# Nearest 2x upsampling on one core: two loads and eight of nine stores move from the SyncE and ScalarE queues to GpSimd, as single packets

## The chip, the cores and the metric

The kernel runs on one core of a Trainium2 chip. The metric is the device time of one execution in microseconds (us), as the median of several runs. A core has compute engines, each with its own instruction queue: TensorE (PE), VectorE (DVE), ScalarE (ACT), GpSimd (POOL) and SyncE (SP). Here only DVE computes. Data move between the off-chip memory (HBM) and the on-chip memory (SBUF, 128 partitions) by 16 DMA engines, which all queues share: an instruction on SP, ACT or POOL only issues a transfer, and a semaphore tells when it has landed.

## The reference

```python
def setup_inputs():
    batch, channels, h, w = (16, 64, 64, 64)
    return {'x': np.random.randn(batch, channels, h, w).astype(np.float32), 'scale_factor': 2}

def reference(x, scale_factor):
    ...
    for i in range(new_h):
        for j in range(new_w):
            src_i = i // scale_factor
            src_j = j // scale_factor
            result[:, :, i, j] = x[:, :, src_i, src_j].copy()
```

Every input value is written four times, twice along the width and twice along the height. 16.78 MB are read and 67.11 MB are written; nothing is calculated.

## The kernel before, in words

The input is seen as 65,536 image rows of 64 floats (256 bytes). Each of the 128 partitions holds 512 consecutive rows, so a partition's share of any run of rows is one contiguous piece of HBM. The output has the same split: one input row becomes two output rows of 128 floats, 1,024 contiguous bytes.

All of the input lies in SBUF at once, in `xt`. It comes in three loads, called A, B and C here: rows 0 to 31, 32 to 287 and 288 to 511 of each partition (`cuts`, lines 195 to 197). All three are issued by SP. The helper `begin_before_barrier` takes the first `EARLY` = 3 transfers of SP out of the body of the program and puts them ahead of SP's part in the barrier at the program's start, so that they are issued at once.

Then come nine groups of rows (`rows`, line 181: 54, 38, 54, 60, 54, 62, 64, 62 and 64). For each, DVE copies the rows into an expanded tile `u`, reading each value twice along the width and each row twice (`expanded`, lines 199 to 202), and one transfer stores `u` to HBM. Copies and stores are numbered 0 to 8 here. Copy 0 is cut in two: its first row alone (line 216), then the other 53 rows (line 217).

There is no separate memory for all the tiles. `u` lies by turns at the start of one large buffer `mem` and just below the unread part of the input (`at`, line 208). So copy n+2 writes where the tile of store n lay, and must wait until store n has landed. Copy 0 waits for load A (its first row) and B; copies 5 and later read rows of load C.

The issuing queue is SP for loads A, B, C and stores 0, 1 and 8, and ACT for stores 2 to 7 (line 218). The transfers of one queue are taken up in their order. Each queue's instruction waits until DVE has finished the tile that it stores.

A transfer over 128 partitions is spread over 16 DMA engines, eight partitions to each. A partition's piece is one packet here: the page counts 1,728 packets for 12 transfers, which is 128 of data and 16 small ones for the semaphore to each.

The helper `close_early` rearranges the end of the program: all engines meet in the closing barrier once their instructions are issued; GpSimd waits for all transfers but the last and clears the semaphores; SP waits only for the last store and resets its semaphore.

Of the kernel before, what the change touches and what calls it, by code (L numbers as in the profile page):

```python
# [6 lines left out]

EARLY = 3  # L10


def begin_before_barrier(nc):
# [5 lines left out]
    sp = mybir.EngineType.SP  # L19
    loads = [i for i in body.instructions if i.engine == sp][:EARLY]  # L20
    for load in loads:
# [132 lines left out]
@with_exitstack  # L154
def kernel(
    ctx: ExitStack,
    tc: tile.TileContext,
    x: bass.AP,
    scale_factor: int,
    out: bass.AP,  # L160
):
    nc = tc.nc
    nc.at_finalize(begin_before_barrier)
    nc.at_finalize(close_early)
    P = nc.NUM_PARTITIONS
    s = int(scale_factor)
    B, C, H, W = x.shape
    R = B * C * H // P
    fdt = x.dtype

    xp = x.rearrange("b c h w -> (b c h) w").rearrange("(p r) w -> p r w", p=P)
    op = out.rearrange("b c (h hd) w -> (b c h) (hd w)", hd=s).rearrange(
        "(p r) w -> p r w", p=P
    )

    rows = [54, 38, 54, 60, 54, 62, 64, 62, 64]
    GROW = s * s
    FREE = 79
    WF = FREE * GROW * W
    assert sum(rows) == R
    mem_pool = ctx.enter_context(tc.tile_pool(name="mem", bufs=1))
    LEAD = 32
    whole = mem_pool.tile([P, LEAD + WF + R * W], fdt, name="mem")
    mem = whole[:, LEAD:]
    xt = mem[:, WF:].rearrange("p (r w) -> p r w", r=R)  # L190

    HEAD = 32
    cuts = [0, HEAD, R // 2 + HEAD, R]
    for lo, hi in zip(cuts, cuts[1:]):
        nc.sync.dma_start(out=xt[:, lo:hi], in_=xp[:, lo:hi])  # L197

    def expanded(r0, r1):
        return (  # L200
            xt[:, r0:r1].unsqueeze(2).unsqueeze(4).to_broadcast([P, r1 - r0, s, W, s])
        )

    r0 = 0
    before = (0, 0)
    for n, k in enumerate(rows):
        size = k * GROW * W
        at = 0 if n % 2 == 0 else WF + r0 * W - size
        assert at >= before[1] or at + size <= before[0]
        before = (at, at + size)  # L210
        u = mem[:, at : at + size].rearrange(
            "p (k a w b) -> p k a w b", k=k, a=s, w=W
        )
        k0 = 1 if n == 0 else 0
        if k0:
            nc.vector.tensor_copy(out=u[:, :k0], in_=expanded(r0, r0 + k0))  # L216
        nc.vector.tensor_copy(out=u[:, k0:], in_=expanded(r0 + k0, r0 + k))  # L217
        issuer = nc.sync if n in (0, 1, len(rows) - 1) else nc.scalar
        issuer.dma_start(out=op[:, r0 : r0 + k, :], in_=u)
        r0 += k  # L220


# [33 lines left out]
```

## Time and profile before

| | us |
|---|---|
| median of 3 runs (196.98 to 197.09) | 197.05 |
| the profiled execution's own time | 197.08 |
| span in the profile | 195.8 |
| DVE busy | 76.9 |
| POOL busy | 0.2 |
| DMA queues' packets (share of 16 engines' span) | 55.0% + 44.2% |
| bytes moved | 83.89 MB, 429 GB/s over the span |

The time is the span and about 1.3 us around it. The span begins with the first instruction, which is the issue of load A. Times of single events below count from there. In the chain of work that ended last, each row gives its start, its length and what it was; a row "DMA" is the time from the issue of a transfer to its landing, as far as an instruction waited for it. In the timeline, each row gives start, length, engine, line, operation and, in brackets, how long the engine had been idle and what ended that. The view by windows gives, for a stretch, the busy time of each engine, the clock of TensorE, the share of the 16 DMA engines' time and the rate; there a packet counts whole at the moment at which it starts, so a stretch in which several packets start has a share above 1.

### The profile page before, as it was taken

The numbers are of one execution on the slowest core, as the hardware profiler recorded it, in microseconds if no ns is written. First come the engines' busy times: TensorE is split into PE (matmuls) and PEld (weight loads), VectorE is DVE, ScalarE is ACT, GpSimd is POOL, SyncE is SP. The second block draws the span as 40 slices with busy tenths as digits, with TensorE's granted clock in tenths as the row PEclk, the third lists the DMA queues.
The fourth block names the chain that finished last, engine by engine and source line by source line (L and its number), as shares of the span: only waits on it lengthen the run. The fifth ranks groups of instructions, "written<-read, shape, count | busy, mean of one in ns | idle before, by whom it ended". The sixth has DMA issues, their size and how long they took to land.

```text
span 195.8 us, 76 instructions
## 1 busy us (share of the span) xinstructions
DVE 76.9 (39%) x10; POOL 0.2 (0%) x4
## 2 busy tenths in 40 slices
DVE  0000099990029287059008805920790079000000
POOL 0000000000000000000000000000000000000000
DMA  9999989989898988999999899999999999999994
GB/s 429 429 429 429 402 375 539 398 362 542 362 435 382 551 373 362 542 402 402 402 537 407 362 542 415 415 415 415 429 429 429 429 415 558 473 435 422 429 429 214
DMA packets 1728, 83.89 MB, mean 429 GB/s; under 512 B 192, under 2 KB 192, under 8 KB 192
## 3 DMA queue, kind: packets, MB, share of 16 engines
q10 hardware_dynamic: 864, 46.66, 55.0%
q1 hardware_dynamic: 864, 37.22, 44.2%
HBM read 16.78 MB, written 67.11 MB: 429 GB/s over the span
## 4 chain that ended last, share of the span: by engine, by line
DMA 61%; DVE 24%; SPq 0%; issue 0%
DMA out_dram<-mem 49%; DVE mem L217 24%; DMA mem<-in_x_dram 12%; SPq L197 0%
## 5 line engine op out<-in xcount | busy, mean ns | idle before, releaser
L217 DVE COPY mem<-mem 128x13824 f32<-128x13824 f32 (+5 forms) x9 | 76.6, 8515 | 84.6 <-DMA out_dram<-mem 65.6
L216 DVE COPY mem<-mem 128x256 f32<-128x256 f32 x1 | 0.3, 293 | 4.8 <-DMA mem<-in_x_dram 4.8
L237 POOL MEMSET const-bfloat16-1.0<- 128x1 bf16 x1 | 0.1, 102 | 0.0
L237 POOL MEMSET const-uint8-127<- 128x1 uint8 x1 | 0.1, 101 | 0.0
L237 POOL MEMSET const-float32-0.0<- 128x1 f32 x1 | 0.1, 98 | 0.2 <-issue 0.2
L237 POOL MEMSET const-float32-1.0<- 128x1 f32 x1 | 0.1, 98 | 0.0
## 6 DMA issues: line engine op xcount, KB each, us to landing
out_dram<-mem ACTq DMA_DIRECT2D x2, 7936.0 KB, 31.6
out_dram<-mem ACTq DMA_DIRECT2D x2, 6912.0 KB, 23.7
out_dram<-mem ACTq DMA_DIRECT2D x1, 7680.0 KB, 26.1
mem<-in_x_dram SPq DMA_DIRECT2D x1, 7168.0 KB, 40.2
out_dram<-mem SPq DMA_DIRECT2D x1, 6912.0 KB, 19.0
out_dram<-mem SPq DMA_DIRECT2D x1, 4864.0 KB, 25.2
mem<-in_x_dram SPq DMA_DIRECT2D x1, 1024.0 KB, 4.8
mem<-in_x_dram SPq DMA_DIRECT2D x1, 23.7
```

What stands on the lines that cost most here:

```text
L216: nc.vector.tensor_copy(out=u[:, :k0], in_=expanded(r0, r0 + k0))
L217: nc.vector.tensor_copy(out=u[:, k0:], in_=expanded(r0 + k0, r0 + k))
L237: nc = _bacc.Bacc("TRN2", target_bir_lowering=False, num_devices=1)
```

## The change

Load A becomes 64 rows and stays on SP. Loads B and C become 224 rows each (64 to 287 and 288 to 511) and are issued by GpSimd, with `single_packet=True`: the eight pieces of each DMA engine form one packet. Stores 0 to 7 are issued by GpSimd too, in the same way. Store 8 stays on SP as it was. ACT issues nothing. `EARLY` becomes 1, since only load A is left ahead of the barrier; GpSimd's loads come after it. The copies on DVE are the same ten instructions. The larger load A now holds all the 54 rows of copy 0, so copy 0 waits for load A alone, and copy 1 is the first to wait for load B.

```diff
-EARLY = 3
+EARLY = 1
...
-    HEAD = 32
-    cuts = [0, HEAD, R // 2 + HEAD, R]
-    for lo, hi in zip(cuts, cuts[1:]):
-        nc.sync.dma_start(out=xt[:, lo:hi], in_=xp[:, lo:hi])
+    HEAD = 64
+    cuts = [0, HEAD, R // 2 + HEAD // 2, R]
+    nc.sync.dma_start(out=xt[:, :HEAD], in_=xp[:, :HEAD])
+    for lo, hi in zip(cuts[1:], cuts[2:]):
+        nc.gpsimd.dma_start(out=xt[:, lo:hi], in_=xp[:, lo:hi], single_packet=True)
...
-        issuer = nc.sync if n in (0, 1, len(rows) - 1) else nc.scalar
-        issuer.dma_start(out=op[:, r0 : r0 + k, :], in_=u)
+        dst = op[:, r0 : r0 + k, :]
+        if n == len(rows) - 1:
+            nc.sync.dma_start(out=dst, in_=u)
+        else:
+            nc.gpsimd.dma_start(out=dst, in_=u, single_packet=True)
```

## The prediction

> **What bounds the kernel now.** I read the page's DMA parts first, then the chain of work that ended last, then the timeline around each store.
>
> ```profile
> q10 hardware_dynamic: 864, 46.66, 55.0%
> q1 hardware_dynamic: 864, 37.22, 44.2%
> HBM read 16.78 MB, written 67.11 MB: 429 GB/s over the span
> DMA 61%; DVE 24%; SPq 0%; issue 0%
> ```
>
> The packets of the two queues fill 55.0% + 44.2% = 99.2% of what 16 DMA engines have in the span. The chain gives DVE 24%, but that is only the way by which the waits lead back; the DMA engines work on underneath. The timeline shows it:
>
> ```profile
> 24.11 19.55 DVE L217 COPY mem<-mem 128x13568 f32<-128x13568 f32 x2 [18.99 <-DMA mem<-in_x_dram]
> 57.46 7.36 DVE L217 COPY mem<-mem 128x13824 f32<-128x13824 f32 x1 [13.80 <-DMA out_dram<-mem]
> 64.85 82.42 ACTq L219 DMA_DIRECT2D out_dram<-mem  x6
> 69.03 8.16 DVE L217 COPY mem<-mem 128x15360 f32<-128x15360 f32 x1 [4.21 <-DMA out_dram<-mem]
> 85.25 7.36 DVE L217 COPY mem<-mem 128x13824 f32<-128x13824 f32 x1 [8.07 <-DMA out_dram<-mem]
> 103.47 8.43 DVE L217 COPY mem<-mem 128x15872 f32<-128x15872 f32 x1 [10.85 <-DMA out_dram<-mem]
> 119.68 8.70 DVE L217 COPY mem<-mem 128x16384 f32<-128x16384 f32 x1 [7.78 <-DMA out_dram<-mem]
> 138.47 8.43 DVE L217 COPY mem<-mem 128x15872 f32<-128x15872 f32 x1 [10.10 <-DMA out_dram<-mem]
> 157.71 8.69 DVE L217 COPY mem<-mem 128x16384 f32<-128x16384 f32 x1 [10.81 <-DMA out_dram<-mem]
> ```
>
> Each copy from 57.46 on starts when an older store lands, so the starts are landings: stores 0 to 6 at 57.46, 69.03, 85.25, 103.47, 119.68, 138.47 and 157.71. Between the first and the last, stores 1 to 6 (332 rows, 43.52 MB) land in 100.25 us: 434 GB/s. The idle time in the brackets is DVE's slack: when copy n is done, store n goes into the queue and the store ahead of it still runs for that long. The smallest such cover is 4.21 us (store 2, issued at 64.85, taken up when store 1 ends near 69). Nothing that DVE does sets the end: the DMA engines do, from the first byte to the last.
>
> So only three things can change the time: what a byte costs inside the engines, what they lose at the start, and a gap if a transfer is not there in time. At the start, and packet by packet:
>
> ```profile
> 0.50:1.00 0.50, 0.00 (x0) 0.00 (x0) 1.00 0.00 0
> 1.00:1.50 0.50, 0.00 (x0) 0.00 (x0) 1.00 1.41 229
> 1.50:2.00 0.50, 0.00 (x0) 0.00 (x0) 1.00 0.49 131
> 2.00:4.00 2.00, 0.00 (x0) 0.00 (x0) 1.00 0.98 414
> 62.48:62.49 0.01, 0.01 (x1) 0.00 (x0) 1.00 26.98 11674
> 192.61:192.62 0.01, 0.00 (x0) 0.00 (x0) 1.00 45.34 19661
> ```
>
> A packet counts whole where it starts, so the last two rows weigh packets. At 62.48, 11674 GB/s x 0.01 us = 116.7 KB are three pieces of store 1 (38 KB); 26.98 x 16 x 0.01 us / 3 = 1.439 us each. At 192.61, 196.6 KB are three pieces of store 8 (64 KB) with 45.34 x 16 x 0.01 / 3 = 2.418 us each. The 26,624 bytes between them take 0.979 us, 36.77 ns per KB of 1,000 bytes; 38,912 bytes at that pace are 1.431 us. Some 8 ns of each packet (within 1 ns, by the last digit) are not bytes.
>
> **The change, part by part.**
>
> *Packets.* Ten transfers (B, C, stores 0 to 7) put eight pieces on each engine. As one packet they would pay the 8 ns once and not eight times: 10 x 7 x 8.1 ns = 0.57 us on every engine, all of it on the path, since the engines never rest. Load A and store 8 keep their eight packets. Bounds: nothing if the 8 ns belong to the piece, and 0.57 us if to the packet. I take the upper end: the two rows show a cost at each boundary, and the change takes the boundary away.
>
> By the Trainium skill's page "DMA: Bandwidth & Descriptors", section "Why small descriptors are slow (HBM only)", a packet costs about three cycles, and packetization saves that but not what belongs to a descriptor. At the 850 MHz that the same page gives in "Where 436 GB/s comes from", three cycles would be 3.5 ns, an estimate of 0.25 us for 70 boundaries, and the sum would be 196.8; the rows show 8 ns, and which part of it is the packet's no row here tells.
>
> *Load A from 32 to 64 rows.* It is first as before. The first 1.05 MB land at 4.83 and A and B together (9.44 MB) at 24.11:
>
> ```profile
> 4.83 0.29 DVE L216 COPY mem<-mem 128x256 f32<-128x256 f32 x1 [4.83 <-DMA mem<-in_x_dram]
> 0.00 0.38 SPq L197
> ```
>
> That is 8.39 MB in 19.28 us, 435 GB/s, so a load A of 2.10 MB lands at 4.83 + 2.41 = 7.2 if nothing gets between. It is the same bytes in the same order and costs nothing.
>
> *Loads B and C on GpSimd, after the barrier.* SP needs 0.38 us for one issue, then the barrier; I put GpSimd's issue at about 0.7. A transfer issued by SP moves its first bytes 1.0 us after its issue (nothing before 1.00 in the windows above). What a GpSimd issue needs no row shows. Its lower bound is SP's 1.0; as its upper bound I take the 2.4 us that load A needs beyond its bytes (4.83 - 2.41). So B's first bytes come between 1.7 and 3.1, while load A keeps the engines busy to about 6.7. The cover is 3.6 us beyond the upper bound; behind it each us costs a us.
>
> *Copy 0* waits for A alone and runs from about 7.5.
>
> ```profile
> L217 DVE COPY mem<-mem 128x13568 f32<-128x13568 f32 x1 | 14.3, 14286 | 19.0 <-DMA mem<-in_x_dram 19.0
> L217 DVE COPY mem<-mem 128x9728 f32<-128x9728 f32 x1 | 5.2, 5226 | 0.0
> ```
>
> Its 53 rows take 14.29 us and the 38 of copy 1 5.23, by the groups by form, so it ends near 22, not at 38.4. Store 0 then lies in the queue behind load C, which ends at 41 as before. This gains nothing, as the engines are full until 41 anyway; what it buys is cover for a slower issue. Copy 1 waits for B (24.1) as DVE's next work, and ends at 29.4.
>
> *Stores 0 to 7 on GpSimd.* Same order, one queue, no store behind a later one's wait: each waits only for its copy, and the one reused load semaphore that store 3 and store 7 also wait for is set long before. An issue slower than ACT's is hidden as long as it takes less than the 4.21 us of store 2's cover less about 1 us of landing; the other stores have 7.8 us or more. Over the upper bound of 2.4 us this holds, so I cost it at nothing. The tiny packet that raises the semaphore is there as before.
>
> *The end.* Store 8 stays on SP, is issued near 166 while store 7 runs, and the engines work both off in either order. GpSimd's clearing is done while store 8 still runs. Nothing.
>
> Sum against the profiled execution (197.08, span 195.8): 197.08 - 0.57 = 196.5. It stands 0.03 above the median of 197.05, so the forecast is **196.5 us**, 0.28% faster. A gain can be larger: between 1.00 and 2.00 the engines move 180 KB where at 414 GB/s it would be 414, a loss of 0.56 us, and a second queue that fills in there could give it back: 196.0.
>
> **The rivals.**
>
> *Load A stuck behind the large packets (slower).* A transfer on a second queue does not wait for the first queue's end. Store 7 went out on ACT, store 8 on SP:
>
> ```profile
> 128.40 18.87 ACTq L219 DMA_DIRECT2D out_dram<-mem  x2
> 166.43 0.33 SPq L219 DMA_DIRECT2D out_dram<-mem  x1
> out_dram<-mem ACTq DMA_DIRECT2D x1, 7936.0 KB, 36.7
> ```
>
> Store 7, issued at 146.9, alone would land 18.7 us (8.13 MB at 434 GB/s) after store 6, at 176.4. It landed at 146.9 + 36.7 = 183.6, so 7.2 us of store 8, three of its 2.42 us packets, went in between: the engines take queues by turns, packet by packet. In the new kernel B's packet on each engine is 57,344 x 8 bytes, 16.9 us at 434 GB/s, and C's the same. If B comes up while packets of A are left, A waits 16.9 us; with two left, it waits for C too, since each turn gives A one packet. Then A lands at 41, copy 0 ends at 55.6, and store 0's bytes come 1.0 to 2.4 us later, with the engines empty from 41: 15.6 us or more. If copy 1 right behind it (5.2 us) also holds GpSimd's issue back, 20.8. Time: 196.5 + 15.6 = 212, up to 218.
>
> For it: A's packets (16 KB, 0.61 us each) run until 6.7, and B comes at 1.7 to 3.1. Against it: the engines choose well ahead. Store 2 was issued at 64.85 into 4.2 us of store 1 and did not delay it at all (69.03 - 57.46 = 11.57 us for 4.98 MB, its own time at 434 GB/s being 11.5); store 8's first packet came only after store 7's sixth, some 4 us after its issue. Counted from 0.7 that gives 4.7, with three packets of A still to be chosen by then if GpSimd's queue is as fast as ACT's, and none if it needs 2 us more. It decides at that point. By my bounds GpSimd's issue takes up to 1.4 us more than SP's, which leaves at most a packet or two to chance; since nothing in the trace decides between these ends, I give the clean start the greater part, but not by much.
>
> The page named above says in "Queues, rings and completion order" that an engine goes round its queues and drains a whole packet before it switches; the trace agrees, by store 7's 36.7 us.
>
> *Store 0's issue waits for DVE.* Only if load A is late, but not behind C: copy 0 would then run from 24.1 to 38.4 as before, copy 1 at once to 43.65, and if GpSimd cannot issue while DVE copies, store 0's bytes start at 44.7 and the engines stand still for 3.6 us: 200.1. It needs A to land after 9.8 (24.1 - 14.3); from about 20 on it costs time. No row here shows a GpSimd issue beside a copy.
>
> It is the rule of the Trainium skill's page "SBUF — State Buffer", section "SBUF: two separate sides", box "The 'DVE blocks DMA' trap (SWDGE)": DVE's fp32 copies lock GpSimd out while it writes descriptors. For stores 1 to 7 the rule would cost nothing here, since DVE's idle times of 4.2 to 13.8 us behind each copy leave room.
>
> *GpSimd's path is slower by itself.* Issue beyond the covers of 3.6 us (load B) or 3.2 us (store 2), or each of its transfers leaving a tenth of a us between itself and the next (ten of them, 1.0 us, which has no cover): 197.5 to 199.
>
> *The 8 ns stay, or the queue eats them.* Then the time is that of before, 197.05.
>
> **How the numbers follow.** This kernel's runs differ by 0.1 us, so 0.2% (0.39 us) is about what can be told from no change. Chances: the clean saving 0.46 (196.0 to 196.65); no net change 0.12; a moderate loss, by the slower path or store 0's wait, 0.23 (197.45 to 201.5); load A behind both packets 0.19 (210 to 218). So faster 0.46, same 0.12, slower 0.42. The likeliest one's own range is 196.0 to 196.7; the range that leaves out the last case and little else is 196.0 to 201.5.
>
> **What would show it.** Right: the first copy of line 218 near 7.5 us and the next near 24; no idle DMA slice; the pieces of stores 0 to 7 at 434 GB/s plus 8 ns per piece less; a span near 195.2. Wrong: the first copy near 24 or 41, and a hole in the DMA row behind 41 us; B's first bytes after 6.7; or the packets' shares adding to what they were, with the span at 195.8. What would make the forecast wrong most surely is load A's place in the turns.

## The result: slower by 0.6%, lost between load C and store 0

The changed kernel takes 198.32 us (198.27 to 198.39), the kernel before 197.07 in the same runs: a ratio of 1.0062, 95% interval 1.005 to 1.0074. The forecast was 196.5 us; its range ran on to 201.5. The span of the profile grew from 195.8 to 197.0 us. First the page of the changed kernel (its DMA packets and queues), then rows of its timeline:

```profile
DMA packets 1728, 83.89 MB, mean 426 GB/s; under 512 B 192, under 2 KB 192, under 8 KB 192
q0 software_dynamic: 1440, 73.40, 86.6%
q1 hardware_dynamic: 288, 10.49, 12.6%
```

```profile
1.31 1.20 POOL L198 DMA_DIRECT2D mem<-in_x_dram  x2 [0.87 <-PEq L255]
13.38 0.29 DVE L217 COPY mem<-mem 128x256 f32<-128x256 f32 x1 [13.38 <-DMA mem<-in_x_dram]
13.59 19.54 DVE L218 COPY mem<-mem 128x13568 f32<-128x13568 f32 x2
28.17 5.08 POOL L223 DMA_DIRECT2D out_dram<-mem  x1 [25.66 <-DVE mem L218]
33.43 0.54 POOL L223 DMA_DIRECT2D out_dram<-mem  x1 [0.18 <-issue]
58.68 7.36 DVE L218 COPY mem<-mem 128x13824 f32<-128x13824 f32 x1 [25.54 <-DMA out_dram<-mem]
66.33 0.53 POOL L223 DMA_DIRECT2D out_dram<-mem  x1 [32.36 <-DVE mem L218]
70.22 8.16 DVE L218 COPY mem<-mem 128x15360 f32<-128x15360 f32 x1 [4.19 <-DMA out_dram<-mem]
158.92 8.69 DVE L218 COPY mem<-mem 128x16384 f32<-128x16384 f32 x1 [10.81 <-DMA out_dram<-mem]
```

Store 0 landed at 58.68 (before: 57.46, 1.22 later), store 1 at 70.22 (1.19 later), store 6 at 158.92 (1.21 later). So nothing is lost after store 0, and the queues' packets still add to 99.2% (86.6% + 12.6%). Windows around the change from loads to stores, called the seam below, show where it went. Each row counts a packet at its start; the first fence is the kernel before, the second the changed one.

```profile
0.00:38.00 38.00, 14.19 (x2) 0.20 (x4) 1.00 0.98 417
38.00:38.90 0.90, 0.86 (x2) 0.00 (x0) 1.00 2.36 1019
40.20:43.00 2.80, 2.80 (x1) 0.00 (x0) 1.00 1.46 632
```

```profile
0.00:38.00 38.00, 19.71 (x3) 7.02 (x8) 1.00 0.98 417
38.00:38.90 0.90, 0.00 (x0) 0.00 (x0) 1.00 3.60 1019
40.20:43.00 2.80, 0.00 (x0) 0.00 (x0) 1.00 0.73 316
```

Up to 38.0 both kernels moved the same: 417 GB/s. In the next 0.9 us the last pieces of load C start in both, one on each of the 16 engines (1019 GB/s x 0.9 us = 16 x 57,344 bytes). Their mean length is the share times the stretch: 2.36 x 0.9 = 2.12 us before, 3.60 x 0.9 = 3.24 after. This stretch on all engines at once is 1.1 of the 1.2 us. Behind it only 16 pieces of store 0 start before 43 (316 GB/s) where 32 did (632).

### The profile page after: what moved, and what is told of

Read it like the earlier page. It is cut to its first block, busy times and chain, and to the rows that moved or that the text cites. A ratio compares the mean times of both kernels' runs of the same rounds, so it can differ in the third digit from the quotient of the medians.

```text
span 197.0 us, 76 instructions
## 1 busy us (share of the span) xinstructions
DVE 76.8 (39%) x10; POOL 10.2 (5%) x14
## 2 busy tenths in 40 slices
DMA packets 1728, 83.89 MB, mean 426 GB/s; under 512 B 192, under 2 KB 192, under 8 KB 192
## 3 DMA queue, kind: packets, MB, share of 16 engines
q0 software_dynamic: 1440, 73.40, 86.6%
q1 hardware_dynamic: 288, 10.49, 12.6%
## 4 chain that ended last, share of the span: by engine, by line
DMA 47%; issue 22%; DVE 13%; POOL 3%; DVEq 0%; POOLq 0%; PEldq 0%
DMA out_dram<-mem 47%; DVE mem L218 13%; POOL out_dram L223 3%; POOL mem L198 1%; DVEq L218 0%; POOLq L223 0%; PEldq L255 0%
## 5 line engine op out<-in xcount | busy, mean ns | idle before, releaser
L223 POOL DMA_DIRECT2D out_dram<-mem x8 | 8.8, 1102 | 137.6 <-DVE mem L218 137.4
L198 POOL DMA_DIRECT2D mem<-in_x_dram x2 | 1.2, 602 | 0.9 <-PEq L255 0.9
```

Of the source, the lines that this page charges most:

```text
L198: nc.gpsimd.dma_start(out=xt[:, lo:hi], in_=xp[:, lo:hi], single_packet=True)
L223: nc.gpsimd.dma_start(out=dst, in_=u, single_packet=True)
```

## The experiments

Three theories at first. P: the packet setting stretches the pieces. G: a load and a store behind each other in GpSimd's queue do it. R: GpSimd has nothing to do with it; the larger load A lets copy 0 end early, store 0 then lies ready while load C is still being read, and that costs 1.2 us.

| kernel | store 0 issued, us | queues of C, store 0 | store 0 landed, us | time, us | ratio to before, 95% |
|---|---|---|---|---|---|
| before | 38.42 | SP, SP | 57.46 | 197.07 | |
| after | 28.17 (to 33.25) | POOL, POOL | 58.68 | 198.32 | 1.005 to 1.0074 |
| multi | 28.27 (to 33.36) | POOL, POOL | 58.66 | 198.22 | 1.0033 to 1.0063 |
| head64_hw | 21.69 | SP, SP | 58.78 | 198.35 | 1.0036 to 1.007 |
| hw_36 | 36.51 | SP, SP | 58.98 | 198.37 | 1.0037 to 1.0067 |
| hw_37 | 37.57 | SP, SP | 58.25 | 197.85 | 1.0027 to 1.0052 |
| hw_38 | 38.83 | SP, SP | 57.63 | 196.99 | 0.9978 to 0.9997 |
| gps_37 | 38.30 | POOL, POOL | 57.41 | 197.01 | 0.9983 to 1.0002 |
| gps_38 | 39.10 | POOL, POOL | 57.60 | 197.48 | 1.0002 to 1.0021 |
| gps_52 | 38.59 | POOL, SP | 58.26 | 197.88 | 1.002 to 1.0045 |
| act01 | 38.33 | SP, ACT | 58.44 | 197.96 | 1.0021 to 1.0045 |
| hw_52 | 38.60 | SP, SP | 57.56 | 197.15 | 0.9987 to 1.0007 |
| early_row | 21.69 | SP, SP | 58.91 | 198.47 | 1.005 to 1.008 |
| loads_sp | 21.89 | SP, POOL | 63.62 | 202.97 | 1.0274 to 1.0305 |
| stores_hw | 28.21 | POOL, SP | 58.46 | 199.45 | 1.0056 to 1.0165 |
| gps_head32 | 40.09 (to 45.18) | POOL, POOL | 62.70 | 202.26 | 1.0211 to 1.0261 |

Each ratio is against runs of the kernel before on the same chip, whose medians lay between 197.07 and 197.36 (single runs between 196.96 and 197.62). The issue and the landing are those of the profiled execution. Where a second time stands, GpSimd's issue took until then.

### The packet setting: multi

```diff
-        nc.gpsimd.dma_start(out=xt[:, lo:hi], in_=xp[:, lo:hi], single_packet=True)
+        nc.gpsimd.dma_start(out=xt[:, lo:hi], in_=xp[:, lo:hi])
...
-            nc.gpsimd.dma_start(out=dst, in_=u, single_packet=True)
+            nc.gpsimd.dma_start(out=dst, in_=u)
```

> The changed kernel without single_packet, all else the same. Theory P (the packet setting causes the stretch of load C's last pieces, 3.3 us where they took 2.1): the hole behind 38.5 us goes, store 0 lands near 57.4, time near 197.1. Theory R (store 0 lies ready in the queue before load C ends, and the change from loads to stores then costs about 1.2 us): nothing changes, 198.3, pieces of the same length as before, load A again at about 13 us. Theory G (a load and a store behind each other in GpSimd's queue cost it): 198.3.

198.22 us, store 0 landed at 58.66, load A at 13.48: the same as with the setting. P falls, and the setting has no effect that these runs show.

### The cuts alone, with no transfer on GpSimd: head64_hw

```diff
-    HEAD = 32
-    cuts = [0, HEAD, R // 2 + HEAD, R]
+    HEAD = 64
+    cuts = [0, HEAD, R // 2 + HEAD // 2, R]
```

> The kernel before with only the cuts changed: load A 64 rows, B and C 224 each, all on SP; no GpSimd transfer. Store 0 is issued near 22 us on SP instead of 38.4. Theory R: the same stretch appears at the end of load C without any GpSimd transfer, time 198.2 to 198.3. Theories P and G: no stretch, 197.0 to 197.1.

The kernel before with nothing but the new cuts takes 198.35 us, ratio 1.0053. Its timeline and windows:

```profile
7.38 14.28 DVE L217 COPY mem<-mem 128x13568 f32<-128x13568 f32 x1
21.69 8.05 SPq L219 DMA_DIRECT2D out_dram<-mem  x2
```

```profile
38.00:38.90 0.90, 0.00 (x0) 0.00 (x0) 1.00 3.78 1019
40.20:43.00 2.80, 0.00 (x0) 0.00 (x0) 1.00 0.73 316
```

Copy 0 ends at 21.7, store 0 is issued 17 us earlier than before, and the last pieces of load C take 3.78 x 0.9 = 3.40 us. The new cuts, set by one number of the change, make the whole loss without GpSimd. P and G fall.

### Loads or stores alone on GpSimd: loads_sp and stores_hw

```diff
 loads_sp (against the changed kernel)
-EARLY = 1
+EARLY = 3
...
-        nc.gpsimd.dma_start(out=xt[:, lo:hi], in_=xp[:, lo:hi], single_packet=True)
+        nc.sync.dma_start(out=xt[:, lo:hi], in_=xp[:, lo:hi])

 stores_hw (against the changed kernel)
-        dst = op[:, r0 : r0 + k, :]
-        if n == len(rows) - 1:
-            nc.sync.dma_start(out=dst, in_=u)
-        else:
-            nc.gpsimd.dma_start(out=dst, in_=u, single_packet=True)
+        issuer = nc.sync if n in (0, 1, len(rows) - 1) else nc.scalar
+        issuer.dma_start(out=op[:, r0 : r0 + k, :], in_=u)
```

> The changed kernel with loads B and C back on SP ahead of the barrier; stores 0 to 7 stay on GpSimd as single packets. Load A should land at 7.2, copy 0 end at 22 and store 0 be issued near 22 without DVE in its way. The engines take queues by turns, so stores 0 may mix with load C. Theory R: a loss of about 1.2 us where C gives way to store 0, or a different one if they mix, 198 or so. Theory G: no load and store share GpSimd's queue, 197.0 to 197.1. Theory P: the stores are still single packets, but load C is not, 197.1.

> The changed kernel with the stores back where they were (0, 1, 8 on SP, 2 to 7 on ACT); loads B and C stay on GpSimd. Load A lands at about 13 again, copy 0 ends at 28, store 0 is issued there on SP while load C is in GpSimd's queue. Theory R: a loss at the change from loads to stores, 198 or so. Theory G: C and store 0 are in different queues, no stretch, 197.1. Theory P: load C is still one packet, 198.3.

Both were meant to separate load C and store 0 into two queues, and both show a second thing with it: the engines then take the two by turns. loads_sp takes 202.97 us (ratio 1.0274 to 1.0305), far from every expectation. Its timeline:

```profile
21.89 0.67 POOL L223 DMA_DIRECT2D out_dram<-mem  x1 [21.45 <-DVE mem L218]
63.62 7.36 DVE L218 COPY mem<-mem 128x13824 f32<-128x13824 f32 x1 [34.36 <-DMA out_dram<-mem]
71.28 0.53 POOL L223 DMA_DIRECT2D out_dram<-mem  x1 [41.17 <-DVE mem L218]
```

Store 0, issued at 21.89, shares the engines with load C and lands at 63.62 where it did at 57.46. Copy 2 waits for it, so store 2 goes out at 71.28 instead of 64.85, when little of store 1 is left:

```profile
25.50:25.80 0.30, 0.30 (x1) 0.00 (x0) 1.00 9.47 2867
70.30:72.30 2.00, 0.68 (x1) 0.53 (x1) 1.00 0.05 19
```

In the 2 us from 70.3 a single piece starts (19 GB/s x 2 us = 38 KB): store 1 is all but over and store 2 not yet there. A transfer that others wait for was slowed by giving its neighbour a turn. The first row is the seam in this run: 15 pieces of load C, just ahead of store 0's first pieces, take 9.47 x 0.3 x 16 / 15 = 3.03 us instead of 2.12. The rest of the 5.6 us (202.97 against 197.36 for the kernel before in the same runs) was not followed up.

stores_hw took 199.45 us in the median, from 198.05 (its profiled execution) to 200.89; that spread is not explained. In the profiled execution store 0 was issued at 28.21 and landed at 58.46, a loss of 1.0 although load C was in another queue. So the loss does not need one queue, which G requires. Its windows show the loss away from the end of load C:

```profile
29.70:30.30 0.60, 0.60 (x1) 0.00 (x0) 1.00 4.70 1529
31.90:32.80 0.90, 0.90 (x1) 0.00 (x0) 1.00 1.82 573
32.80:33.40 0.60, 0.60 (x1) 0.00 (x0) 1.00 1.49 645
```

16 pieces of load C take 4.70 x 0.6 = 2.82 us and the next nine 1.82 x 0.9 x 16 / 9 = 2.91, together 1.1 us more per engine than at 2.12. Then store 0's first pieces come in the third row (seven, of the usual 2.04 us). So in these two runs, as in the changed kernel, the load pieces that are stretched are the one or two just ahead of a large store's first piece on each engine, at the end of load C or in its middle.

### When store 0 is issued: hw_36, hw_37 and hw_38

The kernel before with the cuts of head64_hw; store 0 is held back by copying the first rows of its tile again behind copy 1 (52 rows in hw_36, 52 and 6 in hw_37, 52 and 14 in hw_38). The second copy reads rows that copy 1 has overwritten, so store 0's values are not the reference's in these three and in gps_37 and gps_38; its bytes and their times are those of the same transfer.

```diff
+        if n == 0:
+            held = u
+            r0 += k
+            continue
+        if n == 1:
+            for again in [52]:
+                nc.vector.tensor_copy(out=held[:, :again], in_=expanded(0, again))
+            nc.sync.dma_start(out=op[:, :r0, :], in_=held)
```

> The kernel before with the cuts at 64 and 288 and no GpSimd transfer, but store 0 held back: DVE copies the first 52 rows of its tile a second time behind copy 1, so that store 0 is issued near 36.4 instead of 21.7 us, 1.8 us ahead of the start of load C's last pieces (38.2). Theory R as it stands now (the loss comes when the engines choose store 0's reads while loads are still being read): they choose some 3 to 4 us ahead of the bytes, so the stretch should be whole or nearly: 198.0 to 198.3. Rival R2 (the loss needs a store that lies ready many us ahead): no stretch, 197.1.

> Between hw_36 and hw_38: store 0 is issued near 37.5 us. Its first rows are copied again from memory that copy 1 has overwritten, as in hw_36, hw_38 and gps_38, so the output of store 0 is not the reference's. If the engines choose store 0 as soon as they have asked for the last bytes of load C, and that happens before 38, the stretch is there in whole or on some engines, 197.4 to 198.3; if its descriptors come too late for that, none, 197.0.

> As hw_36, with 14 rows more copied again, so that store 0 is issued near 38.4 us, as in the kernel before. Theories R and R2: the stretch is gone and the time is that of before, 197.0 to 197.4. Rival C (the cuts themselves, 64/224/224 rows, cost the 1.2 us): 198.3 as in head64_hw.

One row of windows each, in the order hw_36, hw_37, hw_38:

```profile
38.00:38.90 0.90, 0.00 (x0) 0.00 (x0) 1.00 3.70 1019
```

```profile
38.00:38.90 0.90, 0.00 (x0) 0.00 (x0) 1.00 3.07 1019
```

```profile
38.00:38.90 0.90, 0.80 (x1) 0.00 (x0) 1.00 2.36 1019
```

The last pieces of load C take 3.33 us when store 0 is issued at 36.51, 2.76 at 37.57 and 2.12 at 38.83. The loss follows the moment of the issue (whole, half and none) within 2.3 us; being ready for many us (R2) is not needed. With the cuts of the slow kernel hw_38 is as fast as the kernel before, so the cuts themselves (rival C) cost nothing.

### The changed kernel with store 0 held back: gps_38 and gps_37

The same insertion in the changed kernel, with `nc.gpsimd.dma_start(..., single_packet=True)`, and 40 rows (gps_38) or 34 rows (gps_37) copied again.

> The changed kernel, with store 0 held back by a second copy of 40 of its rows behind copy 1, so that GpSimd issues it near 38.6 us with DVE idle. Theory R: the stretch is gone and with it the whole loss, 197.0 to 197.4, GpSimd's queue costing nothing by itself. If GpSimd's issue is too slow for what is left of load C (to 40.4), a gap of up to 1 us. Theory C or G: 198.3.

> gps_38 with store 0 issued by GpSimd 0.8 us earlier, near 38.3 us. If the 0.2 us that gps_38 still lost at the seam came from an issue that was late, the seam now costs less, 197.2 to 197.4; if it is now early enough to be chosen while load C is read, part of the stretch is back, up to 198.3.

gps_37, in its timeline and windows:

```profile
38.30 0.54 POOL L226 DMA_DIRECT2D out_dram<-mem  x1 [35.79 <-DVE mem L225]
57.41 7.36 DVE L218 COPY mem<-mem 128x13824 f32<-128x13824 f32 x1 [19.41 <-DMA out_dram<-mem]
```

```profile
38.00:38.90 0.90, 0.00 (x1) 0.60 (x2) 1.00 2.36 1019
```

197.01 us: with loads B and C and eight stores on GpSimd as single packets, and store 0 issued at 38.30, the time is that of the kernel before (ratio 0.9992, interval 0.9983 to 1.0002), the last pieces of load C take 2.12 us and store 0 lands at 57.41. GpSimd's queue costs nothing by itself, and gains nothing. DVE's work is not the cause either: DVE is idle at 38 us in hw_36, with the stretch, and in gps_37, without it, and busy in hw_38, without it (the first busy time in each row). gps_38, issued 0.8 us later, took 197.48 where the kernel before took 197.24 in the same runs, and store 0 landed 0.19 us later than in gps_37: there the issue came a little late. What it lost after store 0 was not followed up.

### Load A at 32 rows, with GpSimd beside a copy: gps_head32

```diff
 (against the changed kernel)
-    HEAD = 64
-    cuts = [0, HEAD, R // 2 + HEAD // 2, R]
+    HEAD = 32
+    cuts = [0, HEAD, R // 2 + HEAD, R]
```

> The changed kernel with load A back at 32 rows and the cuts of before (32, 288): copy 0 waits for load B, ends near 38.4, and copy 1 follows at once to 43.6. If GpSimd cannot issue while DVE copies, store 0's issue ends near 43.8, its bytes start about 2 us later, and the engines stand still from 41 on for some 4 to 5 us: 201 to 202. If DVE's copy does not hold it back: 197.1 to 197.4.

202.26 us, just above the range that was expected if DVE's copy holds the issue back; ratio 1.0211 to 1.0261. In its timeline and windows:

```profile
25.51 19.55 DVE L218 COPY mem<-mem 128x13568 f32<-128x13568 f32 x2 [20.55 <-DMA mem<-in_x_dram]
40.09 5.09 POOL L223 DMA_DIRECT2D out_dram<-mem  x1 [37.58 <-DVE mem L218]
62.70 7.36 DVE L218 COPY mem<-mem 128x13824 f32<-128x13824 f32 x1 [17.64 <-DMA out_dram<-mem]
```

```profile
41.00:42.20 1.20, 1.20 (x1) 1.20 (x1) 1.00 0.00 0
42.20:45.70 3.50, 2.85 (x1) 3.33 (x2) 1.00 0.00 0
```

Store 0's issue takes 5.09 us where the others take 0.53, and ends at 45.18, 0.12 us after copy 1 (25.51 + 19.55 = 45.06). No packet starts from 41.0 to 45.7, and store 0 lands 5.2 us later than before. In the changed kernel the same thing happens at 28.17 (5.08 us, with copy 1 ending at 33.13), but load C covers it. The box on the "DVE blocks DMA" trap in the Trainium skill's page "SBUF — State Buffer", section "SBUF: two separate sides", tells of this lock; the trace agrees, and shows its price: the rest of the copy. Load B also landed late here (copy 0 starts at 25.51, not 24.11). Load A, of 32 rows, had landed at 4.66, when some of B's first pieces had not yet started; how the 1.4 us come about was not followed up.

### A small store early: early_row

```diff
 (against head64_hw)
+            nc.scalar.dma_start(out=op[:, r0 : r0 + k0, :], in_=u[:, :k0])
...
-        issuer.dma_start(out=op[:, r0 : r0 + k, :], in_=u)
+        issuer.dma_start(out=op[:, r0 + k0 : r0 + k, :], in_=u[:, k0:])
```

> The kernel of head64_hw (cuts 64 and 288, all transfers on SP and ACT, store 0 issued near 21.7), and the first output row pair of each partition (1 KB, 0.13 MB in all) goes out by itself on ACT near 7.5 us, while loads B and C are being read. Theory once (the first store that is chosen while loads are still being read costs 1.2 us, and no later one): a lag of 1.2 us behind the kernel before already at 12 us, none added at 41 us, 198.3. Theory each (every change from loads to stores costs it): 1.2 us at 8 to 12 and 1.2 us more at 41, 199.5. Theory size (it needs large stores): nothing at 8, 1.2 at 41, 198.3.

198.47 us, store 0 landed at 58.91. In its windows:

```profile
0.00:38.00 38.00, 19.72 (x3) 0.20 (x4) 1.00 0.99 421
38.00:38.90 0.90, 0.00 (x0) 0.00 (x0) 1.00 3.66 1019
```

Up to 38 us nothing is lost (421 GB/s, 417 in the kernel before), though a store was among the loads; the last pieces of load C take 3.66 x 0.9 = 3.29 us (3.40 in head64_hw). "Once" and "each" both fall: the 1 KB pieces cost nothing, the 54 KB pieces that follow the whole.

### Two queues: gps_52, act01 and hw_52

```diff
 gps_52 (against the changed kernel)
-    HEAD = 64
-    cuts = [0, HEAD, R // 2 + HEAD // 2, R]
+    HEAD = 52
+    cuts = [0, HEAD, 288, R]
...
-        if n == len(rows) - 1:
+        if n in (0, 1, len(rows) - 1):

 act01 (against the kernel before)
-        issuer = nc.sync if n in (0, 1, len(rows) - 1) else nc.scalar
+        issuer = nc.sync if n == len(rows) - 1 else nc.scalar

 hw_52 (against the kernel before)
-    HEAD = 32
-    cuts = [0, HEAD, R // 2 + HEAD, R]
+    HEAD = 52
+    cuts = [0, HEAD, 288, R]
```

> The changed kernel with load A of 52 rows (B 236, C 224) and stores 0 and 1 on SP as before; B, C and stores 2 to 7 stay on GpSimd as single packets. Copy 0 needs row 53 and so waits for load B again (24.1 to 38.4), and store 0 is issued near 38.4 us by SP, beside copy 1. If the loss is store 0's early issue, and GpSimd's queue costs nothing: no stretch at the end of load C, 197.0 to 197.2, the kernel before within 0.1%. If the queue costs something by itself: above 197.5. Nothing is expected to be gained over the kernel before.

> The kernel before with stores 0 and 1 on ACT, so that load C (SP) and store 0 (ACT) stand in different queues; store 0 is issued near 38.4 us as before, and GpSimd moves nothing. Theory two queues: store 0's first pieces are long, 2.7 to 3.1 us, and the time is 197.8 to 198.0. Theory GpSimd (its queue for load C makes them long) or cuts: no stretch, 197.0 to 197.3.

> The kernel before with the cuts of gps_52 (52 and 288) and nothing else: all on SP and ACT, store 0 behind load C in SP's queue, issued near 38.5. Theory two queues, theory GpSimd, and the theory of the early issue: 197.0 to 197.3, no stretch. Theory cuts: 197.8.

gps_52 was meant as the repair and missed: 197.88 us, with store 0 issued at 38.59. Its windows, and then two rows of act01:

```profile
38.00:38.90 0.90, 0.86 (x2) 0.00 (x0) 1.00 2.35 1019
40.20:43.00 2.80, 2.80 (x1) 0.00 (x0) 1.00 1.03 316
```

```profile
38.00:38.90 0.90, 0.86 (x2) 0.00 (x0) 1.00 2.61 1019
40.20:43.00 2.80, 2.80 (x1) 0.00 (x0) 1.00 1.02 316
```

In gps_52 the last pieces of load C are normal (2.35 x 0.9 = 2.12 us) and the first 16 pieces of store 0 are long: 1.03 x 2.8 = 2.88 us, where 55,296 bytes take 2.04 (in the kernel before, 1.46 x 2.8 / 2). act01 has the same (2.86 us) with no transfer on GpSimd, 197.96 us, and its last pieces of load C are a little long as well (2.61 x 0.9 = 2.35 us); hw_52, with the cuts of gps_52 and one queue, has 197.15. So it is not GpSimd and not the cuts: with load C in one queue and store 0 in another, store 0 lands 0.8 (gps_52) and 1.0 us (act01) later than in the kernel before, even at the right moment of issue.

What happens inside the engines is not settled. What the runs agree on is this: the first large store behind the loads costs 0.6 to 1.3 us on every engine if it is issued 0.6 us or more ahead of the start of the last pieces of load C, or in another queue than load C; and it costs 0.2 us or less, by its landing, if it is issued in the same queue from 38.3 on, when those pieces have begun to start. That the engine's reads of the store's tile come in the way of its reads of the load would fit the moment, but no record shows reads and writes apart, and it would not explain why two queues at 38.3 lose and one does not.

## Why the prediction was wrong

**The step that failed** is in the part on copy 0: "This gains nothing, as the engines are full until 41 anyway; what it buys is cover for a slower issue". A store that waits behind a load was taken to be free, and so the term was put at nothing; it cost 1.2 us at the seam. The engines were never empty there, but the pieces themselves took longer. With this term and without the gain of the next paragraph the prediction's own sum gives 197.08 + 1.2 = 198.3, the measured time. Nothing in the trace of before showed that seam otherwise than at its best: store 0 was issued at 38.42, just behind the start of load C's last pieces; 1 to 2 us earlier (hw_37, hw_36) the loss would have stood in it. None of the rivals had it. The slower side was forecast at 0.42, but from other causes: that 198.3 lies among the prediction's moderate losses is luck.

**Packets: 0.57 us of gain, measured nothing.** It was the term for the forecast, taken at its upper bound. That the setting joins eight pieces to one packet, as the description of the change has it, no run shows: the page after counts 1,728 packets as before, and a window of the changed kernel weighs a piece of store 1 on GpSimd:

```profile
59.48:59.49 0.01, 0.01 (x1) 0.00 (x0) 1.00 8.99 3891
```

3891 GB/s x 0.01 us is one piece of 38.9 KB, and 8.99 x 16 x 0.01 = 1.438 us, as before. The 8 ns stay on every piece; the lower of my two bounds was right, and multi shows the setting to do nothing. Whether the 8 ns belong to the piece, or the setting joined no pieces, no run tells. The estimate of 0.25 us worked out from the Trainium skill's page "DMA: Bandwidth & Descriptors" did not come out either.

**Load A stuck behind the large packets.** A landed at 13.38, not 7.2 (7.17 in head64_hw, where one queue has all loads): 6.2 us late, three pieces of B at 2.1. The queues did take turns as this rival said, but piece by piece, not by packets of 16.9 us, so its price of 15.6 us did not come. By the rule of the Trainium skill's page "DMA: Bandwidth & Descriptors", section "Queues, rings and completion order", a whole packet is drained before the switch; the eight pieces were not one packet in this sense, and the measurement decides. Copy 0 started at 13.6 and was still far ahead of time.

**B's first bytes between 1.7 and 3.1: measured 5.5 to 6.3.** GpSimd's two issues start at 1.31, not 0.7, and take 0.6 us each; the windows of the changed kernel:

```profile
5.00:5.40 0.40, 0.00 (x0) 0.00 (x0) 1.00 0.38 164
5.45:5.50 0.05, 0.00 (x0) 0.00 (x0) 1.00 4.17 1802
```

164 GB/s x 0.4 us are four pieces of A (16 KB); 1802 x 0.05 = 90.1 KB are two of A and the first of B. By 6.3 every engine had a piece of B and none had stood idle, so the cover held. In gps_head32, where A is half as long, B's first pieces start from 3.8 us on, 2.5 us after the issue began.

**Stores on GpSimd, hidden: right.** An issue takes 0.53 us and starts 0.28 us after its copy (78.40 to 78.68 in the chain of waits, for store 3); store 2's cover of 4.19 us held it, and store 1 to store 8 run as before. gps_37 shows the whole queue to be neutral. **Store 0's wait for DVE** came by its mechanism: the issue at 28.17 took 5.08 us, until copy 1 was over. It cost nothing here, since A landed between the 9.8 and the 20 us that this rival names; gps_head32 pays for it, with 202.26 us where the rival had 200.1.

## What to carry to other kernels

Where the DMA engines are full from end to end, look for a change of their time at the seams, between loads and stores, before blaming the engine that issues: give windows of a few tenths of a us to the last packets of the one and the first of the other, and compare their mean lengths. A store that is ready early is not free there; in this kernel the good moment was when the last pieces of the load had begun, in the load's own queue. And an experiment that sets only the smallest part of a change (here one number, the cuts) can carry the whole result.

## What the runs showed of the hardware that was not expected

- The seam, with load and store in one queue: the last 57 KB pieces of a load take 3.2 to 3.4 us in the mean of the 16 engines instead of 2.12 when a store of 54 to 55 KB pieces was issued 1.7 us or more ahead of them, 2.76 at 0.6 us (hw_37), and 2.12 at 0.1 us behind the first one's start (gps_37).
- With the store in another queue and issued in the middle of the load, the load pieces just ahead of the store's first are stretched there: 1.1 us per engine at 30 to 33 us in stores_hw, 0.9 at 25.5 in loads_sp.
- With the store in another queue and issued at the end of the load, its own first pieces take 2.9 us instead of 2.04 (act01, gps_52).
- `single_packet` on GpSimd changes neither the length of a piece (1.438 us of 38.9 KB) nor the turns between queues (load A lands at 13.38 with it and at 13.48 without).
- A GpSimd issue beside a running copy lasts until 0.12 us after the copy's end: 5.1 us instead of 0.53.
